# Larger target pieces, one larger pred piece and statistics ahead of subtractions in a masked-autoencoder loss kernel

## The chip, the cores and the metric

One NeuronCore of a Trainium2 chip runs the whole program. The metric is device time in microseconds (us), the median of several runs. The engines are named as the profile names them: PE (TensorE), DVE (VectorE), ACT (ScalarE), POOL (GpSimd), SP (SyncE).

## The reference

```python
# pred, target: (32, 147, 768) float32, norm_pix_loss = True
mean = target.mean(axis=-1, keepdims=True)
var = target.var(axis=-1, keepdims=True)
target = (target - mean) / np.sqrt(var + 1e-6)
loss = np.mean((pred - target) ** 2, axis=-1)
return loss.mean(axis=-1).astype(np.float32)      # (32,)
```

## The kernel before

The 32 x 147 rows are laid out as 36 columns of 128 rows and a rest of 96 rows ("column 36"). Each row has 768 numbers. For a column c, DVE makes the statistics of the target (two `bn_stats` of 384 and a `bn_aggr`), ACT the root, DVE the reciprocal, GpSimd the normalised target `s`. The difference `pred - s` is made on PE (two products with plus and minus the identity, added in PSUM, the memory that PE writes to) or on DVE (a subtraction); it is squared and summed on ACT or on DVE. At the end small matmuls add the sums over rows.

All but the first two transfers cast float32 to bfloat16 and are issued by GpSimd. A `piece` is one transfer, of target ("t") or pred ("p"). The list of pieces from target column 16 on, and the units of work for the last columns:

```python
    piece("t", 16, 20)
    piece("t", 20, 24)
    piece("p", 4, 8)
    piece("t", 24, 28)
    piece("t", 28, 32)
    piece("p", 8, 12)
    piece("t", 32, 36)
    for c in range(12, 24, 4):
        piece("p", c, c + 4)
    for c in range(24, 32, 2):
        piece("p", c, c + 2)
    for c in range(32, 35):
        piece("p", c, c + 1)
    piece("p", KM - 1, KM, 0, half)
    piece("p", KM - 1, KM, half, D)
    # ... cut ...
    units += [((24,), 0, D, "DVE"), ((25,), 0, D, "DVE+ACT")]
    # "DVE": subtraction and square on DVE. "DVE+ACT": subtraction on DVE, square on ACT.
    # from 26 on: the first 512 numbers of a column on PE and ACT, the last 256 on DVE
```

The kernel is recorded as a list of operations with guessed durations, and a small scheduler in the kernel's own code puts them in an order, engine by engine. Of two operations that could start at the same moment, the one of lower rank goes first.

Of the kernel before, what the change touches and what calls it, by code (L numbers as in the profile page):

```python
# [14 lines left out]
def kernel(  # L15
# [19 lines left out]
    REST = KM  # L35
# [4 lines left out]
    def rows_of(c):  # L40
        return RP if c == REST else P
# [12 lines left out]
    def piece(kind, c0, c1, d0=0, d1=D, q="sw"):  # L54
        stream.append((kind, c0, c1, d0, d1, q))
# [5 lines left out]
    piece("p", REST, REST + 1)  # L61
    piece("t", 12, 16)
    piece("p", 0, 4)
    piece("t", 16, 20)
    piece("t", 20, 24)
    piece("p", 4, 8)
    piece("t", 24, 28)
    piece("t", 28, 32)
    piece("p", 8, 12)
    piece("t", 32, 36)  # L70
    for c in range(12, 24, 4):
        piece("p", c, c + 4)
    for c in range(24, 32, 2):
        piece("p", c, c + 2)
    for c in range(32, 35):
        piece("p", c, c + 1)
# [20 lines left out]
    def op(name, engine, dur, needs, fn, rank=0.0, early=0.0):  # L97
        by_name[name] = len(ops)
        ops.append((name, engine, dur, needs, fn, rank, early))
# [17 lines left out]
    for i, (kind, c0, c1, d0, d1, q) in enumerate(stream):  # L117
# [3 lines left out]
        for c in range(c0, c1):  # L121
            land[kind, c, d0] = clock + 1.1
        k = len(lanes[q])
        op(("load", i), {"hw": "SP", "hw2": "ACT", "sw": "POOL"}[q], 0.6, [], lambda a=stream[i]: load(*a), rank=-1.0,
           early=0.0 if k <= 8 else lanes[q][k - 9] + 0.3)

    def landed(kind, c):
        return max(t for (k, cc, d), t in land.items() if k == kind and cc == c)
# [27 lines left out]
    def bn(out, parts):  # L156

        n = parts[0].shape[0]
        st = small.tile([P, len(parts), 6], F32, name="st")
        for j, x in enumerate(parts):  # L160
            pin(nc.vector.bn_stats(out=st[:n, j, :], in_=x))  # L161
        pin(nc.vector.bn_aggr(out=out, in_=st[:n, :len(parts)]))  # L162

    def stats(g, i):
        n, K = rows_of(g[0]), len(g)
        if i == 0:
            mvs[g] = small.tile([P, K, 2], F32, name="mv")
        if not norm_pix_loss:
            return
        (_, _, til, o), = tbuf[g[i]]  # L170
        bn(mvs[g][:n, i], [til[:n, o + a:o + a + half] for a in (0, half)])

    def root(g):
        n, K = rows_of(g[0]), len(g)
        r = small.tile([P, K], F32, name="r")
        nm = small.tile([P, K], F32, name="nm")
        for i, c in enumerate(g):
            rs[c] = (r[:n, i:i + 1], nm[:n, i:i + 1])
        rs[g] = r
        if not norm_pix_loss:  # L180
            pin(nc.vector.memset(r, 1.0))
            pin(nc.vector.memset(nm, 0.0))
            return
        mv = mvs[g]
        pin(nc.scalar.activation(out=r[:n], in_=mv[:n, :, 1], func=ACTF.Sqrt, bias=eps_t[:n], scale=1.0))  # L185
        pin(nc.scalar.activation(out=nm[:n], in_=mv[:n, :, 0], func=ACTF.Copy, scale=-1.0))  # L186

    def recip(g):
        n = rows_of(g[0])
        if norm_pix_loss:  # L190
            pin(nc.vector.reciprocal(out=rs[g][:n], in_=rs[g][:n]))  # L191

    for k, g in enumerate(groups):
        for i, c in enumerate(g):
            op(("bn", c), "DVE", 1.26, [], lambda g=g, i=i: stats(g, i), rank=k - 50.0 if c < 32 or c == REST else -1.5, early=landed("t", c))
        op(("root", k), "ACT", 0.55, [("bn", c) for c in g], lambda g=g: root(g), rank=-1.0)
        op(("recip", k), "DVE", 0.2, [("root", k)], lambda g=g: recip(g), rank=-60.0)

# [70 lines left out]
        pin(nc.vector.scalar_tensor_tensor(out=z, in0=z, scalar=1.0, in1=z, op0=ALU.mult, op1=ALU.mult,  # L269
                                           accum_out=dest))  # L270

    tail = 6
    n_early = len(units) - 1 - tail
    rl = singles.tile([P, n_early], F32)
    rl_sum = singles.tile([P, 1], F32)
# [6 lines left out]
    for k, (u, d0, d1, eng) in enumerate(units):  # L282
# [17 lines left out]
        if eng in ("DVE", "DVE+ACT"):  # L300
            op(("diff", k), "DVE", 0.57 * w / D + 0.05, norms + dusers[-5:-4] + dprev[-1:], lambda u=u, d0=d0, w=w: difference(u, d0, w), rank=-2.0,
               early=arrive)
# [12 lines left out]
           early=arrive)  # L315
# [15 lines left out]
    for i, (need, vec, m, n) in enumerate(finals):  # L331
        op(("final", i), "PE", 0.2, [need, "masks"], lambda v=vec, m=m, n=n: final(v, m, n), rank=90.0,
           early=max(land.values()) + 0.4)
# [6 lines left out]
    while left:  # L340
        best = None
        for i in left:
            name, engine, dur, needs, fn, rank, early = ops[i]
            if any(x not in end for x in needs):
                continue
            t = max([free[engine], early] + [end[x] + (0.0 if ops[by_name[x]][1] == engine else HOP) for x in needs])
# [4 lines left out]
        _, i, t = best  # L351
        name, engine, dur, needs, fn, rank, early = ops[i]
# [43 lines left out]
```

## Time and profile before

| | before |
|---|---|
| time | 76.85 us, median of 3 runs (76.81 to 77.18) |
| span of the profiled execution | 75.1 us |
| busy: DVE, POOL, ACT, PE | 75%, 71%, 40%, 39% |
| bytes read | 28.90 MB |
| end of the stream of transfers | about 71.2 us |
| end of DVE's last square | 72.64 us |

The time is about 1.75 us longer than the span. The lines of the profile are read in the prediction below. A "landing" is the moment at which an instruction that waited for a transfer starts. A timeline line has start, duration, engine, source line, operation, output and inputs, shapes, and in brackets the idle time before it with what ended it.

### The profile page before, as it was taken

What the parts mean: (1) busy time and instruction counts of PE and PEld (TensorE: products, weight loads), DVE (VectorE), ACT (ScalarE), POOL (GpSimd) and SP (SyncE); (2) the same over time, 40 slices, a digit from 0 to 9 for tenths busy, and PEclk for the clock granted to TensorE, in tenths of its full rate; (3) what the DMA queues carried; (4) which work ended last, traced back from release to release, by engine and by line L of the source; (5) the groups of instructions that cost most, each with busy time, mean ns of one, the idle gap of its engine ahead of it and who ended that gap; (6) DMA issues with size and microseconds to landing.
All of it is one profiled execution on the core that took longest, in us unless ns stands there. A gap on an engine that the chain in (4) does not pass through costs nothing.

```text
span 75.1 us, 551 instructions
## 1 busy us (share of the span) xinstructions
PE 29.0 (39%) x81; PEld 8.3 (11%) x82; DVE 56.3 (75%) x155; ACT 30.4 (40%) x65; POOL 53.7 (71%) x75
## 2 busy tenths in 40 slices
PE   0000000385004989405973006740709300379760
PEld 0000000011001233002121002110103000112130
DVE  0000399999999999999959999375797389998870
ACT  5100001400202696020690010890099969965950
POOL 6998103999499989398989898987695999900000
PEclk9999999999999999999999755599555797555995
DMA  0799999999999999999999999999999999999900
GB/s 0 196 425 317 234 265 218 193 226 213 219 222 209 219 217 209 209 216 213 209 226 219 220 209 219 209 209 213 213 209 232 196 212 214 213 204 208 148 0 0
DMA packets 3685, 15.41 MB, mean 205 GB/s; under 512 B 418, under 2 KB 1154, under 8 KB 3554
## 3 DMA queue, kind: packets, MB, share of 16 engines
q0 software_dynamic: 3424, 13.52, 89.0%
q1 hardware_dynamic: 258, 1.87, 6.9%
q14 instruction: 3, 0.02, 0.1%
HBM read 28.90 MB, written 0.00 MB: 385 GB/s over the span
## 4 chain that ended last, share of the span: by engine, by line
DMA 51%; POOL 32%; issue 7%; DVE 3%; ACT 2%; PE 2%; POOLq 0%
DMA p<-in_pred_dram 29%; POOL s L211 25%; DMA t<-in_target_dram 22%; POOL p L111 4%; ACT zp L249 2%; POOL t L111 2%; DVE zd L269 2%; PE zp L228 1%; DVE zd L265 1%; POOL ident L139 0%; POOL nident L139 0%; PE acc L328 0%; DVE ob L359 0%; POOL nident L138 0%; POOL ident L138 0%
## 5 line engine op out<-in xcount | busy, mean ns | idle before, releaser
L161 DVE BATCH_NORM_STATS2 st<-t 128x6 f32<-128x384 bf16 (+2 forms) x74 | 36.2, 530 | 10.4 <-DMA t<-in_target_dram 10.4
L211 POOL TENSOR_SCALAR s<-t,nm,r 128x768 bf16<-128x768 bf16 (+2 forms) x37 | 38.3, 1043 | 6.2 <-DVE r L191 5.5
L228 PE MATMUL z<-p,ident 128*128 128x512 bf16 (+2 forms) x23 | 10.4, 614 | 18.3 <-DMA p<-in_pred_dram 18.3
L228 PE MATMUL z<-s,nident 128*128 128x512 bf16 (+2 forms) x23 | 9.8, 546 | 16.2 <-POOL s L211 14.9
L249 ACT ACTIVATE z<-z 128x1536 f32<-128x1536 f32 (+1 forms) x8 | 10.9, 1357 | 11.6 <-PE z L228 11.6
L185 ACT ACTIVATE r<-mv,eps_t 128x4 f32<-128x4 f32 (+2 forms) x11 | 3.2, 292 | 27.4 <-DVE mv L162 26.6
L265 DVE TENSOR_TENSOR zd<-p,s 128x1536 bf16<-128x1536 bf16 (+4 forms) x14 | 9.6, 701 | 3.6 <-DMA p<-in_pred_dram 3.5
L111 POOL DMA_DIRECT2D p<-in_pred_dram x16 | 9.1, 570 | 3.5 <-DMA t<-in_target_dram 1.3
L162 DVE BATCH_NORM_AGGREGATE mv<-st 128x2 f32<-128x12 f32 (+1 forms) x37 | 7.7, 208 | 1.3
L249 ACT ACTIVATE zd<-zd 128x1536 bf16<-128x1536 bf16 (+1 forms) x6 | 8.2, 1364 | 0.7 <-DVE zd L265 0.7
L228 PEld LDWEIGHTS <-ident 128*128 128x128 bf16 (+1 forms) x33 | 4.4, 134 | 33.4 <-issue 33.1
L228 PE MATMUL zp<-p,ident 128*128 128x512 bf16 (+1 forms) x9 | 4.3, 519 | 6.9 <-DMA p<-in_pred_dram 6.9
L228 PEld LDWEIGHTS <-nident 128*128 128x128 bf16 (+1 forms) x33 | 3.5, 122 | 29.7 <-issue 16.6
L249 ACT ACTIVATE zp<-zp 128x1024 f32<-128x1024 f32 (+2 forms) x7 | 5.1, 735 | 1.5 <-PE zp L228 1.4
L111 POOL DMA_DIRECT2D t<-in_target_dram x8 | 4.7, 612 | 1.1 <-DMA t<-in_target_dram 1.1
L228 PE MATMUL zp<-s,nident 128*128 128x512 bf16 (+1 forms) x10 | 4.7, 571 | 2.1 <-ACT z L249 1.7
L269 DVE SCALAR_TENSOR_TENSOR zd<-zd 128x512 bf16<-128x512 bf16 (+3 forms) x8 | 5.0, 623 | 0.2
L186 ACT ACTIVATE nm<-mv 128x4 f32<-128x4 f32 (+2 forms) x11 | 2.1, 189 | 0.0
L185 ACT ACT_TABLE_LOAD x1 | 1.3, 1283 | 0.8 <-PEq L377 0.8
L249 ACT ACTIVATION_READ_ACCUMULATOR z<-z 128x1 f32 (+1 forms) x8 | 1.5, 190 | 0.0
L191 DVE RECIPROCAL r<-r 128x4 f32<-128x4 f32 (+2 forms) x11 | 1.4, 128 | 0.1
L249 ACT ACTIVATION_READ_ACCUMULATOR zp<-zp 128x1 f32 x7 | 1.3, 188 | 0.0
(25 smaller groups left out, 7.0 us busy)
## 6 DMA issues: line engine op xcount, KB each, us to landing
t<-in_target_dram POOLq DMA_DIRECT2D x8, 768.0 KB, 23.7
p<-in_pred_dram POOLq DMA_DIRECT2D x6, 768.0 KB, 29.0
t<-in_target_dram SPq DMA_DIRECT2D x1, 1536.0 KB, 8.0
p<-in_pred_dram POOLq DMA_DIRECT2D x4, 384.0 KB, 24.5
p<-in_pred_dram POOLq DMA_DIRECT2D x3, 192.0 KB, 16.4
t<-in_target_dram SPq DMA_DIRECT2D x1, 288.0 KB, 10.6
p<-in_pred_dram POOLq DMA_DIRECT2D x2, 96.0 KB, 9.5
p<-in_pred_dram POOLq DMA_DIRECT2D x1, 144.0 KB, 13.2
```

The lines of the kernel that those rows point to most:

```text
L111: pin(eng.dma_start(out=til[:n], in_=src))
L161: pin(nc.vector.bn_stats(out=st[:n, j, :], in_=x))
L162: pin(nc.vector.bn_aggr(out=out, in_=st[:n, :len(parts)]))
L185: pin(nc.scalar.activation(out=r[:n], in_=mv[:n, :, 1], func=ACTF.Sqrt, bias=eps_t[:n], scale=1.0))
L186: pin(nc.scalar.activation(out=nm[:n], in_=mv[:n, :, 0], func=ACTF.Copy, scale=-1.0))
L191: pin(nc.vector.reciprocal(out=rs[g][:n], in_=rs[g][:n]))
L211: pin(nc.gpsimd.tensor_scalar(out=s[:n, so:so + D], in0=til[:n, o:o + D], scalar1=nm, scalar2=r, op0=ALU.add, op1=ALU.mult))
L228: pin(nc.tensor.matmul(z[:n, zo + a:zo + b], eye[:n, :n], src[:n, o + a:o + b], start=first, stop=not first))
L249: pin(nc.scalar.activation(out=z[:n, :w], in_=z[:n, :w], func=ACTF.Square, accum_out=dest[:n]))
L265: pin(nc.vector.tensor_tensor(out=x, in0=y, in1=v, op=ALU.subtract))
L269: pin(nc.vector.scalar_tensor_tensor(out=z, in0=z, scalar=1.0, in1=z, op0=ALU.mult, op1=ALU.mult, accum_out=dest))
```

## The change

It makes fewer and larger transfers in the middle of the stream, and keeps DVE on statistics until there are none left. Two sums more (`tail`) are left out of the early total.

```diff
-    piece("t", 16, 20)
-    piece("t", 20, 24)
+    piece("t", 16, 24)
     piece("p", 4, 8)
-    piece("t", 24, 28)
-    piece("t", 28, 32)
+    piece("t", 24, 32)
     piece("p", 8, 12)
     piece("t", 32, 36)
-    for c in range(12, 24, 4):
+    for c in range(12, 28, 4):
         piece("p", c, c + 4)
-    for c in range(24, 32, 2):
+    for c in range(28, 32, 2):
         piece("p", c, c + 2)
 # ... cut ...
-            op(("bn", c), ..., rank=k - 50.0 if c < 32 or c == REST else -1.5, ...)
+            op(("bn", c), ..., rank=k - 50.0 if c < 36 or c == REST else -1.5, ...)
 # ... cut ...
-    tail = 6
+    tail = 8
```

More of the change, by code (lines that the diff above doesn't have):

```diff
@@ L194 @@
         for i, c in enumerate(g):
-            op(("bn", c), "DVE", 1.26, [], lambda g=g, i=i: stats(g, i), rank=k - 50.0 if c < 32 or c == REST else -1.5, early=landed("t", c))
+            op(("bn", c), "DVE", 1.26, [], lambda g=g, i=i: stats(g, i), rank=k - 50.0 if c < 36 or c == REST else -1.5, early=landed("t", c))
         op(("root", k), "ACT", 0.55, [("bn", c) for c in g], lambda g=g: root(g), rank=-1.0)
```

## The prediction

> **What bounds the kernel now.** I read the page's forty slices first, for the engine that never rests.
>
> ```profile
> DVE  0000399999999999999959999375797389998870
> POOL 6998103999499989398989898987695999900000
> DMA  0799999999999999999999999999999999999900
> HBM read 28.90 MB, written 0.00 MB: 385 GB/s over the span
> ```
>
> The DMA engines are full from about 3 us to 71 us. The kernel must read 28.90 MB and nothing in the change alters that. VectorE (DVE) and GpSimd (POOL) are busy 75% and 71%, with holes, so they matter only where they hold up the stream or finish after it. Next I fixed the landing times from the timeline, at instructions whose wait for a DMA was the last:
>
> ```profile
> 53.09 0.96 DVE L265 TENSOR_TENSOR zd<-p,s 128x1536 bf16<-128x1536 bf16 x1 [1.28 <-DMA p<-in_pred_dram]
> 56.74 0.96 DVE L265 TENSOR_TENSOR zd<-p,s 128x1536 bf16<-128x1536 bf16 x1 [0.40 <-DMA p<-in_pred_dram]
> 60.42 3.53 DVE L265 TENSOR_TENSOR zd<-p,s 128x1536 bf16<-128x1536 bf16 x4 [1.61 <-DMA p<-in_pred_dram]
> 64.07 0.58 PE L228 MATMUL zp<-p,ident 128*128 128x512 bf16 x1 [5.17 <-DMA p<-in_pred_dram]
> 65.92 1.01 PE L228 MATMUL zp<-p,ident 128*128 128x512 bf16 x2 [1.27 <-DMA p<-in_pred_dram]
> 67.79 1.01 PE L228 MATMUL zp<-p,ident 128*128 128x512 bf16 x2 [0.43 <-DMA p<-in_pred_dram]
> ```
>
> These are the landings of pred 12, 16, 20 (pieces of four columns) and 26, 28, 30 (pieces of two). Four columns take 3.65 to 3.68 us (1.573 MB read, so about 428 GB/s), two take 1.85. So pieces of two cost the stream nothing against pieces of four. Last, the end, from stretches of 0.2 us and the chain of waits:
>
> ```profile
> 70.80:71.00 0.20, 0.20 (x2) 0.08 (x1) 0.20 (x1) 0.20 (x1) 0.00 (x0) 1.00 0.74 104
> 71.20:71.40 0.20, 0.20 (x2) 0.01 (x2) 0.20 (x1) 0.20 (x3) 0.00 (x0) 1.00 0.03 4
> ...
> 71.68 0.37 DVE zd L265
> 72.07 0.58 DVE zd L269 x2
> 72.70 0.23 PE acc L328 x2
> 72.95 0.18 DVE ob L359
> ```
>
> The last column of the first two rows is GB/s: the stream stops at about 71.2 us. The last subtraction starts at 71.68, not for a wait but because DVE finished the square before it at 71.64. From there to the end of the span (75.1) all is fixed: square, small matmul, copy, store. So at most some 0.4 us lie between stream and end that a better order could win; a DVE that falls behind costs its full amount.
>
> **What the Trainium skill says.** "DMA: Bandwidth & Descriptors", section Where 436 GB/s comes from, gives a ceiling of 435.2 GB/s for the SBUF side of the 16 DMA engines; 428 here agrees, so the stream has under 2% left. The same page, Anatomy of one DMA, gives each transfer a fixed part of about 2.0 us, mostly the wait until the last byte is confirmed. With transfers queued behind one another this trace doesn't show it as lost rate (3.65 against 3.68 above), so three transfers fewer should win next to nothing. "SBUF — State Buffer", section Who interferes with whom, says that a DVE instruction with two SBUF inputs contends with a GpSimd instruction that reads SBUF, and that the later one blocks fully. The trace agrees:
>
> ```profile
> 61.22 1.86 POOL L211 TENSOR_SCALAR s<-t,nm,r 128x768 bf16<-128x768 bf16 x1
> 62.26 1.22 DVE L265 TENSOR_TENSOR zd<-p,s 128x768 bf16<-128x768 bf16 x1
> 63.63 1.96 POOL L211 TENSOR_SCALAR s<-t,nm,r 128x768 bf16<-128x768 bf16 x1
> 64.75 1.11 DVE L265 TENSOR_TENSOR zd<-p,s 128x512 bf16<-128x512 bf16 x1
> 66.51 0.42 DVE L265 TENSOR_TENSOR zd<-p,s 128x512 bf16<-128x512 bf16 x1
> ```
>
> A normalisation on GpSimd is 0.98 us beside statistics and 1.86 to 1.96 beside subtractions and squares; a 512-wide subtraction is 0.42 alone and 1.11 behind a normalisation. One collision costs DVE about 0.69 us.
>
> **The change, part by part.** The order of the stream by columns is unchanged, so piece ends keep their times; only when a column counts as landed moves.
>
> *Target 16-23 and 24-31 as pieces of eight.* Columns 16-19 count as landed only with 20-23. Pred 4 landed at 34.72 (the matmul that waited for it) and follows that piece directly, so the piece lands at 34.72 - 3.67 = 31.05. DVE reached column 16 at 28.29 before, so it now idles some 2.7 us, less the reciprocal it does meanwhile. Eight columns at 1.13 us (start to start in the timeline) end near 40.3. The second piece lands at 45.72 (pred 8) - 3.67 = 42.05: 1.7 us idle, where before it idled 0.82 at 38.36. Then it doesn't stop: 24-31 until 51.4, and 32-35, landed at 49.35, until 56.1. Before, it idled 1.72 at 49.35 and 1.28 at 53.09, made one subtraction (0.96) ahead of the last two columns and ended statistics at 56.34. So statistics end within 0.3 us of before, and the idle time has only moved.
>
> *Statistics ahead of subtractions.* The subtraction for 14/15 runs after 56.1 instead of at 53.09. Those for 16/17 and 18/19 follow at once, ending near 59.3 (three of 0.93, a reciprocal, a short collision); before, 58.81. Pred 20 lands at 60.42, so it is absorbed. ScalarE's squares shift from 56.0 to about 57.1 and it ends pair 22 near 64.9, where it did at 64.33; absorbed by the end.
>
> *GpSimd* gets the reciprocals of 16-19 about 2.9 us later (36.9 for 34.02) and waits for the second big piece before it can issue pred 30 (42.05), since a transfer reuses the semaphore of the one eight issues earlier in the built program. It reaches column 28 at about 53.7, where before 29 started at 53.88: about one normalisation behind. It saves three issues at 0.55, of which two were before 20 us. Its last issue, the second half of column 35, falls near 63.5, and the stream needs it near 70.7: no starvation.
>
> *Pred 24-27 in one piece.* This is the part on the path. Before, columns 24 and 25 landed near 62.26 (60.42 + 1.84) and their two 768-wide subtractions ran by 63.95, with square 24 at 63.87. Now all four land at 64.07. Subtractions 22 end near 62.5, then DVE idles until 64.07. What it has from then on, with start-to-start times of the trace (subtraction 768 0.53, 512 0.45, 384 0.39, 256 0.32; square 768 0.88, 512 0.62, 384 0.50, 256 0.35): subtractions 2 x 0.53 + 3 x 0.45 + 2 x 0.32 + 2 x 0.39 = 3.83; squares 0.88 + 3 x 0.62 + 2 x 0.35 + 0.50 + 0.57 = 4.51; the sum over columns 0.10. Together 8.44, so 72.51 with neither idle time nor collision, against 72.64 for its last square before. Of the normalisations, 34 and 35 probably fall after 64.07 (GpSimd is up to one behind, and stretched by 0.9 at each collision since 56): 1 or 2 collisions, 0.69 to 1.38. That is 73.2 to 73.9, or 0.6 to 1.25 later than before.
>
> *tail 8 for 6* takes column 32's two results out of the sum over columns: two small final matmuls more, about 0.06 us each start to start, while PE waits; it lets that sum run before square 32 is counted. Neutral, or 0.1 us won.
>
> Sum: span 75.1 + 0.6 to 1.25. As all here is a hand-made order of events, I temper it towards no change: +0.75, which gives 76.85 + 0.75 = 77.6.
>
> **Rivals.** (1) GpSimd is not behind, and its last normalisations fall into DVE's new idle time between 62.5 and 64.07. Then the end is 72.5 to 72.8, bound by the landing at about 71.25 as now: 76.7 to 77.0. For it: the change saves GpSimd issue time and a wait of 0.69 at 58.18 for a reciprocal. Against: its long waits at 31 and 42. (2) The stream gets faster through fewer and longer transfers: 21 GpSimd transfers for 24. If each of three saved even 0.1 us, 76.5. Against: 1.85 us for two columns and 3.68 for four. (3) Collisions cascade: every subtraction from 56 on alternates with a normalisation, and subtraction 22 ends after 64.07. Then DVE ends near 74.5: 78.7. For it: three subtractions run back to back beside columns 30 to 32. Against: before, normalisations lost to the next DVE operation rather than alternating strictly. (4) Stream starved by a late issue: several us. Against: 7 us of margin at the last issue.
>
> **Range and chances.** Rival 1 sets the lower side and rival 3 the upper; both have DVE ends a few tenths away from my sum. 2% are 1.54 us, so slower needs rival 3 or 4, and faster needs a stream quicker than anything shown. Chances: faster 0.02, within 2% 0.86, slower 0.12.
>
> **What would show it.** DVE idle before column 16 until about 31.05 and before column 24 until about 42.05; none at column 32; statistics done near 56.1. Pred 24 landing at 64.07 and the stream ending at 71.2, both within 0.2. DVE idle for over 1 us before 64.07, then no idle time until its last square, which ends at 73.2 to 73.9. One or two of the subtractions after 64.07 stretched by 0.7. I am wrong if the stream ends at another time, if GpSimd is done before 64.5, or if DVE again waits for the last landing.

## The result, and the profile after

| | before | after |
|---|---|---|
| time | 76.86 us, median of 6 runs (76.66 to 77.18) | 77.56 us, median of 6 runs (77.48 to 77.69) |
| span of the profiled execution | 75.1 us | 75.8 us |
| last square of DVE ends | 72.64 us | 73.30 us |

The ratio is 1.0089, with a 95% interval of 1.0066 to 1.0112: a loss of 0.9%, within 2% and clear of noise. A ratio here is the mean time of one kernel's runs over that of the other's of the same rounds, so it is not quite the ratio of the medians.

The page of the changed kernel, its forty slices and its bytes:

```profile
DVE  0000699999999960799990999999999892999970
POOL 6998006997398999695594399899999999600000
DMA  0899999999999999999999999999999999999400
HBM read 28.90 MB, written 0.00 MB: 381 GB/s over the span
```

The stream is as full as before and no shorter. DVE now has its holes near 30 and 41 us, and one near 63 us that was not there. The landings, from its timeline:

```profile
52.80 1.44 PE L226 MATMUL z<-p,ident 128*128 128x512 bf16 x3 [2.83 <-DMA p<-in_pred_dram]
63.78 0.58 PE L226 MATMUL zp<-p,ident 128*128 128x512 bf16 x1 [4.06 <-DMA p<-in_pred_dram]
65.65 1.01 PE L226 MATMUL zp<-p,ident 128*128 128x512 bf16 x2 [1.29 <-DMA p<-in_pred_dram]
67.49 1.01 PE L226 MATMUL zp<-p,ident 128*128 128x512 bf16 x2 [0.83 <-DMA p<-in_pred_dram]
```

These are pred 12, 26 (with all of 24 to 27), 28 and 30. Each is 0.2 to 0.3 us earlier than before, and so is pred 12, ahead of which the same bytes have gone; this execution's stream was ahead from the start (the first target landed at 8.21 us where it landed at 8.79). From that first landing to the end of the stream are some 62.8 us, before 62.4: three transfers fewer won next to nothing. All fourteen traces together show a little more. From the landing of pred 4 to that of pred 8 lies one merge: the nine kernels with pieces of eight take 10.91 to 10.93 us, the five with fours 11.00 to 11.03; up to pred 12 the difference is mostly gone (18.26 to 18.38 against 18.31 to 18.32). From pred 12 to pred 26 it is 10.96 to 11.00 us with the single piece and 11.03 to 11.04 without. So a merge wins under 0.1 us.

The end, from stretches of 0.2 us (the last column is GB/s) and from the chain of waits:

```profile
70.80:71.00 0.20, 0.20 (x2) 0.01 (x1) 0.20 (x2) 0.20 (x1) 0.00 (x0) 0.50 0.18 23
...
72.43 0.28 DVE zd L263
72.74 0.58 DVE zd L267 x2
73.36 0.23 PE acc L326 x2
73.62 0.18 DVE ob L357
```

The stream ends at about 71.0 us. DVE's last subtraction starts at 72.35 in the timeline, 1.35 us later; before, it was 71.68 against 71.2. So the end is no longer near the landing: DVE has a backlog. Where it comes from is in the timeline just after pred 24 lands:

```profile
63.75 0.98 POOL L209 TENSOR_SCALAR s<-t,nm,r 128x768 bf16<-128x768 bf16 x1
63.86 2.24 DVE L263 TENSOR_TENSOR zd<-p,s 128x768 bf16<-128x768 bf16 x1 [1.44 <-DMA p<-in_pred_dram]
64.72 0.98 POOL L209 TENSOR_SCALAR s<-t,nm,r 128x768 bf16<-128x768 bf16 x1
66.02 0.55 DVE L263 TENSOR_TENSOR zd<-p,s 128x768 bf16<-128x768 bf16 x1
```

The two lines of POOL are the normalisations of columns 34 and 35, the last two there are. DVE's subtraction for column 24 came 0.11 us after the first of them and took 2.24 us, where the same subtraction for column 25 took 0.55: it waited through both, 1.69 us in all. (e7, the same kernel but for `tail`, repeats it: 0.13 us after the first, and 2.22 us.)

### The profile page after: what moved, and what is told of

Same layout as the page of the kernel before. It is cut to its first block, busy times and chain, and to the rows that moved or that the text cites. A ratio compares the mean times of both kernels' runs of the same rounds, so it can differ in the third digit from the quotient of the medians.

```text
span 75.8 us, 556 instructions
## 1 busy us (share of the span) xinstructions
PE 29.4 (39%) x85; PEld 7.9 (10%) x86; DVE 57.7 (76%) x155; ACT 30.4 (40%) x65; POOL 52.6 (69%) x72
## 3 DMA queue, kind: packets, MB, share of 16 engines
q0 software_dynamic: 2992, 13.52, 87.4%
## 5 line engine op out<-in xcount | busy, mean ns | idle before, releaser
L209 POOL TENSOR_SCALAR s<-t,nm,r 128x768 bf16<-128x768 bf16 (+2 forms) x37 | 38.9, 1059 | 7.4 <-DVE r L189 6.9
L263 DVE TENSOR_TENSOR zd<-p,s 128x1536 bf16<-128x1536 bf16 (+4 forms) x14 | 11.8, 868 | 1.8 <-DMA p<-in_pred_dram 1.7
L109 POOL DMA_DIRECT2D p<-in_pred_dram x15 | 8.6, 572 | 4.6 <-DMA t<-in_target_dram 2.4
L109 POOL DMA_DIRECT2D t<-in_target_dram x6 | 3.8, 631 | 0.0
```

Of the source, the lines that this page charges most:

```text
L109: pin(eng.dma_start(out=til[:n], in_=src))
L209: pin(nc.gpsimd.tensor_scalar(out=s[:n, so:so + D], in0=til[:n, o:o + D], scalar1=nm, scalar2=r, op0=ALU.add, op1=ALU.mult))
L263: pin(nc.vector.tensor_tensor(out=x, in0=y, in1=v, op=ALU.subtract))
```

## The experiments

Twelve kernels ran, in three jobs; each was timed in five rounds beside the kernel before (76.95, 76.85 and 77.03 us in the three jobs), and the changed kernel was not run again with them. "T" is the theory of the prediction: the single piece for pred 24 to 27 makes DVE idle, and its bunched work then meets the last normalisations. The rivals are that the pieces of eight alone put GpSimd behind (R1), or that the new order of statistics costs (R2).

### Each part undone or done alone

**e1: the changed kernel with pred 24 to 27 in two pieces again.**

```diff
-    for c in range(12, 28, 4):
+    for c in range(12, 24, 4):
         piece("p", c, c + 4)
-    for c in range(28, 32, 2):
+    for c in range(24, 32, 2):
```

> The changed kernel with pred 24 to 27 again in two pieces of two. Theory T (the single piece makes VectorE idle until all four columns land and pushes its subtractions 24 and 25 into GpSimd's last normalisations): most of the loss goes, 0.5 to 0.9 us below the changed kernel's 77.56, so 76.7 to 77.1; subtraction 24 starts near 62.4 to 62.6. Rival R1 (the pieces of eight put GpSimd behind, and its late normalisations collide whatever pred does): 77.3 to 77.6. Rival R2 (statistics ahead of subtractions is what costs): 77.3 to 77.6.

Measured: 76.79 us, ratio 0.9979 (0.9962 to 0.9996). The whole loss is gone, and a little more. The single piece is necessary for the loss. R1 and R2 fall as sole causes. (A lower granted clock of PE is no cause either: the runs of e1 took 76.72 to 76.83 us at mean clocks of 0.789 to 0.832, those of e7 below 77.56 to 77.77 at 0.795 to 0.831.)

**e2: the kernel before with that single piece alone** (the same edit the other way round).

> The kernel before with pred 24 to 27 in one piece, nothing else. T: most of the loss appears, 77.2 to 77.6, with VectorE idle before about 63.9 and none after it. R1: 76.8 to 77.0, since GpSimd is not put behind. R2: 76.8 to 77.0.

Measured: 77.06 us, ratio 1.0008 (0.9988 to 1.0029). That is 0.06 us by the ratio, not the 0.3 to 0.7 that was expected. The expectation failed, and its timeline shows why (the profiled execution, 77.20, is the slowest of the six, with its stream some 0.2 us later than in the kernel before):

```profile
63.32 0.97 POOL L211 TENSOR_SCALAR s<-t,nm,r 128x768 bf16<-128x768 bf16 x1
64.32 0.56 DVE L265 TENSOR_TENSOR zd<-p,s 128x768 bf16<-128x768 bf16 x1 [1.76 <-POOL s L211]
```

GpSimd's last normalisation, that of 35, is over at 64.29. The subtraction for column 24 starts 0.03 us later and meets nobody. (The profile names POOL as what ended its wait, since that came last; PE's first product from the same piece waited for the transfer until 64.27, so it was the landing.) DVE was idle for 1.76 us and still lost next to nothing. So the single piece is not sufficient: the idle time alone is cheap.

**e3: the kernel before with the pieces of eight alone.**

> The kernel before with targets 16 to 31 in two pieces of eight, nothing else. T: idle time of VectorE moves to before columns 16 and 24 and the end stays: 76.7 to 77.1. R1: 77.3 to 77.6.

Measured: 77.22 us, ratio 1.0040 (1.0021 to 1.0058). Between the two expectations: 0.3 us. The scheduler moved the reciprocal of columns 32 to 35 behind the subtraction for 20, so that all four of the last normalisations ran from 62.92 to 69.35 us beside DVE's work.

**e4: the kernel before with statistics ahead of subtractions alone.**

> The kernel before with statistics of columns 32 to 35 ahead of subtractions, nothing else (tail left at 6). T: the subtraction for 14 and 15 moves behind the statistics and is absorbed in the idle time before pred 20 lands: 76.7 to 77.1. R2: 77.3 to 77.6.

Measured: 76.92 us, ratio 0.9999 (0.9981 to 1.0016). Nothing, as T said. In e1, where it comes with the pieces of eight, the 0.3 us of e3 are not seen.

**e7: the changed kernel with `tail = 6`.**

> The changed kernel with tail 6. T: neutral, 77.4 to 77.7. Rival (two more final matmuls are what costs): 77.2 or less.

Measured: 77.67 us, ratio 1.0103 (1.0080 to 1.0126). Neutral against the changed kernel's 1.0089, whose interval overlaps.

So of the parts alone, only the pieces of eight cost anything clear of noise, and the sum of the parts, 0.06 + 0.31 - 0.01 = 0.36 us by the ratios, is about half of the 0.68 us that they cost together (1.0089 of 76.86). `tail = 8` was not run alone on the kernel before.

### Is it the collision?

**e5 and e6: the changed kernel, and the kernel before, without the normalisations of 34 and 35.** The result is wrong: columns 34 and 35 subtract the normalised columns 30 and 31. (The comparison with the reference did not notice; the loss averages over all the elements, and other random data give nearly the same mean.)

```diff
+        if c in (34, 35):
+            sbuf[c] = sbuf[30 + c % 2]
+            return
         (_, _, til, o), = tbuf[c]
         r, nm = rs[c]
         pin(nc.gpsimd.tensor_scalar(...))
```

> The changed kernel without GpSimd's normalisations of columns 34 and 35 (they subtract columns 30 and 31 instead, a wrong result on purpose). In the changed kernel's trace the first subtraction after 63.86 takes 2.24 us, as long as these two normalisations run. T with the collision: that subtraction takes about 0.55, VectorE gains 1.7 and is then bound by the last landing again, so the end comes 1.1 to 1.4 us earlier: 76.1 to 76.5. T without the collision (the bunched work of VectorE alone): 77.3 to 77.6.

> The same in the kernel before (wrong result on purpose), as the control. Its last subtraction starts some 0.4 us after the stream ends, so it can win at most that: 76.4 to 76.8. If both kernels then agree within 0.2 us, the difference between them is these two collisions; if the changed one stays 0.5 or more above, it is the bunched work.

Measured: e5 76.60 us, ratio 0.9966 (0.9941 to 0.9991), close to the range; e6 76.96 us, ratio 1.0005 (0.9978 to 1.0032), outside it. For the changed kernel this settles it: with idle time and bunched work left as they are, and only two instructions of GpSimd gone, some 0.95 us go (1.0089 to 0.9966), more than the whole loss and less than the 1.1 to 1.4 that were expected. The three subtractions from 63.95 on took 1.36 us, against 3.05.

The control missed: the kernel before wins nothing. Its timeline shows DVE done at 72.66 and other engines not:

```profile
71.09 0.58 ACT L252 ACTIVATE zp<-zp 128x512 f32<-128x512 f32 x1 [0.45 <-PE zp L231]
...
72.07 1.16 PE L331 MATMUL acc<-mask,rl 128*1 128x32 f32 x12
...
73.27 0.18 DVE L362 COPY ob<-acc 1x32 f32<-1x32 f32 x1 [0.60 <-PE acc L331]
```

ACT waited 0.45 us for PE, and PE's last matmuls ran at a granted clock of 0.50 (in the kernel before it was 1.00 in the stretch from 71 to 73 us). PE had the product of -s for column 34, which needs a free PSUM buffer, ahead of the product of pred 33. The kernel before has the same order, at a clock of 0.86 in the stretch from 69 to 71 us where e6 has 0.50, so order and clock are not separated here. In the changed kernel PE does each column's two products together, and e5 shows no such wait; that this helps was not tested.

DVE itself had next to nothing to win. In e6 it waited 0.67 and 0.73 us for pieces of pred and still ended when it did before (72.64). A line of e8, below, shows the last landing itself:

```profile
71.61 0.36 DVE L261 TENSOR_TENSOR zd<-p,s 128x384 bf16<-128x384 bf16 x1 [0.16 <-DMA p<-in_pred_dram]
```

In that execution the transfers stopped moving data at about 71.2 us, so the waiting subtraction started some 0.4 us after. In the kernel before they stopped between 71.2 and 71.3, and the last subtraction started at 71.68: at the landing, by the same delay. It also started 0.12 us after the accumulator read of the square ahead of it (71.56), where in the changed kernel it starts together with that read (72.35). By the same estimate the backlog of the changed kernel is 1.35 less 0.4, some 0.95 us, which is what e5 won.

**e11: the changed kernel with GpSimd's last issue behind the last two normalisations.** Only one instruction of 0.56 us is moved, the issue of the second half of column 35.

```diff
-           early=0.0 if k <= 8 else lanes[q][k - 9] + 0.3)
+           early=0.0 if k <= 8 else lanes[q][k - 9] + (6.0 if i == len(stream) - 1 else 0.3))
```

> The changed kernel with GpSimd's last issue (second half of column 35, 0.56 us, needed only near 70) behind normalisations 34 and 35 instead of ahead of them; VectorE's order is the same. They should then run from about 63.15 to 65.1 instead of 63.75 to 65.7, and subtraction 24, which comes at about 63.9, be let in 0.6 earlier. By the collision: 0.4 to 0.6 below the changed kernel, 76.9 to 77.2. If the collision isn't what costs: 77.4 to 77.7.

Measured: 76.72 us (76.50 to 76.89), ratio 0.9966 (0.9943 to 0.9988). That is more than expected: 0.95 us by the ratios. It is also a correct version that beats both kernels, the kernel before by 0.3%. Its timeline:

```profile
63.44 0.97 POOL L209 TENSOR_SCALAR s<-t,nm,r 128x768 bf16<-128x768 bf16 x1
64.13 0.69 DVE L263 TENSOR_TENSOR zd<-p,s 128x768 bf16<-128x768 bf16 x1 [1.45 <-DMA p<-in_pred_dram]
64.40 1.92 POOL L209 TENSOR_SCALAR s<-t,nm,r 128x768 bf16<-128x768 bf16 x1
```

The subtraction came 0.69 us after the normalisation of 34 had started, not 0.11. It waited 0.14 us (0.69 against 0.55), and this time it was the normalisation of 35 that had to wait, 1.92 for 0.98. DVE paid 0.6 us a little later, when a square of 0.95 took 1.57, so the collision as a whole cost it some 0.75 us and not 1.69. The phase of two instructions, shifted by 0.6 us, decides over 0.9 us.

### Do the costs add, and who waits for whom?

**e9: before with the single piece and the pieces of eight. e10: before with the single piece and statistics first.**

> The kernel before with both the single piece for pred 24 to 27 and the pieces of eight, but its own order of statistics and tail 6. Alone they cost +0.1 (run e2) and +0.4 (e3) by the ratios. If costs add: 77.3 to 77.4. If what matters is that VectorE comes back from idle time at about 64 while GpSimd runs normalisations back to back and is let in only at the end of their run (in the changed kernel it waited for both): here four of them, 32 to 35, start near 62.9, so it waits up to 2.8 us: 77.6 to 78.4.

> The kernel before with the single piece for pred 24 to 27 and statistics ahead of subtractions, targets in fours, tail 6. Alone they cost +0.1 and 0.0 (e2, e4). If costs add: 76.9 to 77.1. By the collision: GpSimd's normalisations 32 to 34 run beside subtractions 16 to 22 as in e4, its last issue follows and then 35 alone, from about 63.9, so subtraction 24 waits once, for about 0.8: 77.2 to 77.5.

Measured: e9 77.24 us, ratio 1.0032 (1.0012 to 1.0052); e10 77.05 us, ratio 1.0019 (0.9995 to 1.0043). e9 refutes a rule that I had formed, that DVE coming out of idle time waits for the whole run of normalisations: four ran back to back from 61.56 to 67.95, the subtraction came at 63.96, 0.92 us into the second, and took 0.57; the third then took 1.77. In e10 it came within 0.02 us of the one normalisation left:

```profile
64.06 1.42 DVE L265 TENSOR_TENSOR zd<-p,s 128x768 bf16<-128x768 bf16 x1 [1.30 <-DMA p<-in_pred_dram]
64.08 0.98 POOL L211 TENSOR_SCALAR s<-t,nm,r 128x768 bf16<-128x768 bf16 x1
```

It lost 0.87 us there, as foreseen, yet its last square ended at 72.77, only 0.13 us later than in the kernel before, which pays for two collisions of its own (the subtractions of 1.22 and 1.11 us that the prediction shows), and the time is within what adding gives, below the 77.2 to 77.5 that the collision was expected to cost. Neither pair reaches the 0.68 us of all parts together; the third pair, with tail 8, is e1.

**e8: the changed kernel with pred 28 to 31 in one piece as well.**

```diff
-    for c in range(12, 28, 4):
+    for c in range(12, 32, 4):
         piece("p", c, c + 4)
-    for c in range(28, 32, 2):
-        piece("p", c, c + 2)
```

> The changed kernel with pred 28 to 31 in one piece as well. In its trace VectorE reaches subtraction 28 at 67.87, after pred 30 landed at about 67.5, so by T the later landing of 28 costs VectorE nothing: 77.5 to 77.8. Rival (a merged piece costs by itself, through the piece): another 0.6 or so, 78.1 or more.

Measured: 77.25 us, ratio 1.0047 (1.0019 to 1.0074), below both expectations. The run is confounded. The scheduler again put the normalisations of 34 and 35 right after that of 33, with the same starts to within 0.01 us as in e11, so the collision of the changed kernel was gone. Against e11, which has that order too, the second merge does cost, 0.6 us by the ratios, and not through DVE:

```profile
68.77 1.01 ACT L245 ACTIVATE zp<-zp 128x1024 f32<-128x1024 f32 x1 [1.48 <-PE zp L224]
...
73.61 0.18 DVE L355 COPY ob<-acc 1x32 f32<-1x32 f32 x1 [0.69 <-PE acc L324]
```

PE gets pred 28 and 30 at once, so ACT waits 1.48 us for the product of 28, and its squares end behind DVE's. I had looked at DVE alone. (PE's granted clock was 0.50 from 71 to 72 us, against 1.00 in e11, so part of the 0.6 may be the clock's.)

### A version meant to be better

**e12: e1 with the square of column 24 on ACT.**

```diff
-    units += [((24,), 0, D, "DVE"), ((25,), 0, D, "DVE+ACT")]
+    units += [((24,), 0, D, "DVE+ACT"), ((25,), 0, D, "DVE+ACT")]
```

> A version meant to beat both: run e1 (the changed kernel with pred 24 to 27 in two pieces) with the square of column 24 on ScalarE instead of VectorE. VectorE loses 0.9 us of work after 64 and should be bound by the last landing; ScalarE gets 0.9 us and has some idle time before its square of 30. Expected 76.4 to 76.7, against 76.79 for e1; 76.8 or more if TensorE and ScalarE set the end by then.

Measured: 78.08 us, ratio 1.0139 (1.0113 to 1.0164), from 4 runs where the others have 6. A clear miss, some 1.2 us above e1 by the ratios. What the scheduler did shows in its timeline:

```profile
71.96 0.27 PE L326 MATMUL acc<-mask,rl_sum 128*1 128x32 f32 x2 [0.88 <-DVE rl_sum L319]
72.16 0.50 PE L226 MATMUL zp<-s,nident 128*128 128x384 bf16 x1
...
73.07 0.47 ACT L247 ACTIVATE zp<-zp 128x384 f32<-128x384 f32 x1 [1.51 <-PE zp L226]
```

It placed the final matmul that needs DVE's early total ahead of column 35's product on PE, while DVE makes that total only after its last subtraction. PE waited, and the last square of ACT with it, at a granted clock of 0.50 to the end. DVE itself started its last subtraction at 71.46, near the landing. Whether the square on ACT pays with a sane order of PE stays open.

## Why the prediction was right, and where it was not

The time, 77.6 predicted and 77.56 measured, was right, and so were its steps up to the landing of pred 24:

- *The stream is unchanged.* Right within 0.1 us a merge, as shown above; "pieces of two cost the stream nothing" was off by some 0.05 us for two pieces against one. The ceiling of 435.2 GB/s was set against the wrong rate: it is for the side of SBUF, while 428 is what is read. GpSimd's queue wrote 13.52 MB for 27.03 read, since it casts, so SBUF got some 214 GB/s by estimate for most of the stream; of the page's forty slices only the third, near the start, where the two transfers without a cast run, shows 425. How much was left can't be read from that ceiling; the test is what the merges won.
- *Idle time of DVE moves to columns 16 and 24.* Right: they started at 30.75 and 41.69 (predicted 31.05 and 42.05, in an execution whose stream ran some 0.25 us earlier). Statistics ended at about 55.45 (56.1), as I had given the reciprocals too much.
- *GpSimd is about one normalisation behind and issues last near 63.5.* Right: 53.65 at column 28, last issue at 63.14. Collisions from 55 to 62 us came (one subtraction of 0.94 took 1.92, one 1.65, one 1.37) and were absorbed in the idle time before pred 24, as foreseen.
- *DVE idles before pred 24 lands.* Right: 1.44 us.
- *One or two collisions, 0.69 to 1.38 us.* The mechanism is right (e5, e11), the size was off: it was one subtraction that waited 1.69 us behind two normalisations.
- *8.44 us of work after the landing.* Too much. From 63.86 to 73.30 are 9.44 us; without the 1.69 that is 7.75. I had taken start-to-start times from the kernel before, where each square follows its own subtraction. In the changed order DVE mostly does another column's square next, and a 512-wide subtraction takes 0.34 us to the next start (67.87 to 68.21) where it took 0.45 (66.51 to 66.96). So the two terms erred by +0.3 to +1.0 and by -0.7, and much of the sum's agreement is luck. The range from the sum was 0.6 to 1.25 us; the 0.75 was set by tempering it.
- *Pred 24 to 27 in one piece is the part on the path.* Half right. Without it there is no loss (e1), but alone it costs 0.06 us (e2). The loss needs GpSimd to be late as well, at just that moment. I had listed an end bound by the landing, with GpSimd not behind, as a rival at 76.7 to 77.0; e11 shows that moving one issue is enough to get it: 76.72. Which of the two came hung on 0.6 us of phase, and the prediction's own steps were off by about as much (56.1 for 55.45, 36.9 for a reciprocal at 36.44): here too it had luck.
- *tail 8 is neutral.* Right (e7).
- *At most 0.4 us lie between the stream's end and the path's, for a better order to win.* As a bound it held: e11 is 0.26 us faster than the kernel before by the ratio. But the reading under it was wrong, that the last subtraction starts "not for a wait". The delay of some 0.4 us from the end of the transfers to the landing, seen in e8, fills that time by estimate, and e6 freed DVE and gained nothing. Where the 0.26 us of e11 come from is open; the merges and the tail of PE and ACT are candidates.

Still open is why, in the changed kernel, the waiting subtraction was not let in between the two normalisations, while in e11 the second normalisation had to wait for it. The subtractions that came early into a normalisation waited through the next as well (0.11 us in the changed kernel, 0.13 in e7), those that came late were let in (0.69 in e11, 0.92 in e9), but no run varies the moment alone. The traces show when each starts and ends, not who asks first.

## What to carry to other kernels

In this kernel, bound by its stream, merging transfers bought under 0.1 us each, but it moved the moment at which a later engine wakes up; ask what else is running at that moment on the port it needs. Parts of a change may cost more together than added up (here 0.68 us against 0.36), so test combinations before one of them is blamed. Where a scheduler orders the instructions, compare the order on every engine for each variant: here a moved issue was worth 0.9 us, and a version with a misplaced final matmul lost 1.2.

## What the Trainium skill lacked or had wrong

- "SBUF — State Buffer", section Who interferes with whom, says that whichever instruction starts first has the shared ports for the whole of it, and that the other blocks (the sentence stands under DVE's two-port modes; the exclusive lock is the section's general rule). It does not say who is let in when the holder's engine has the next one ready. Here a DVE subtraction that came 0.11 us into a GpSimd normalisation waited through two, 1.69 us; one that came 0.69 us in waited 0.14, and the second normalisation waited instead. In e10 the subtraction started 0.02 us ahead of the normalisation by the trace, and it was the subtraction that waited, 0.87 us.
- "VectorE: DVE Perf Modes", section The DRAIN you can't avoid, reports that a semaphore between DVE instructions, eight copies, costs nothing extra. It gives no figure for an instruction that needs the result of the one before. Here a 512-wide subtraction takes 0.45 us to the start of the square of its own result and 0.34 to the start of another column's square; no run separates a semaphore's part in that.
- "DMA: Bandwidth & Descriptors", section Where 436 GB/s comes from, says that for transfers from HBM the limit of about 358 GB/s per core binds. Here, with one core running, four columns take 3.65 to 3.68 us, some 428 GB/s. The same page, under its table of measured rates, keeps the lower figure for two cores that stream at once; so the skill has it, and only this sentence is wrong for one core.
- The same page's fixed part of about 2.0 us for a transfer does not show as lost rate when transfers are queued: in the kernel before, two pieces of two columns took 3.65 and 3.72 us, one piece of four 3.65 and 3.68. What shows is the delay at the very end: some 0.4 us from the last data moved (about 71.2 us in e8) to the start of the subtraction that waited for it (71.61).
